# A hybrid decoder step in float32 pairs: attention scores of two heads in two row tiles of TensorE, and q and k spilled once

## The chip, the cores and the metric

The kernel runs on one core of a Trainium2 chip. The metric is the device time of one launch in microseconds (us), as the median of repeated runs. A run that was profiled also has a span, from its first to its last instruction, and a trace of every instruction on the five engines: TensorE (PE in the profile, PEld for its weight loads), VectorE (DVE), ScalarE (ACT), GpSimd (POOL) and SyncE (SP), which here only issues DMAs.

## The reference, cut to what matters

One layer of a decoder is computed for a prompt of 1024 positions and for 8 samples of 8 new positions: an RMSNorm, one input projection that is split into a convolution branch and 12 attention heads of 64 channels, the heads' attention, an output projection, a convolutional feed-forward block and a last norm. The part that the change touches is the attention of the prompt: each head attends in three dilated windows, and the three outputs are merged by their softmax denominators.

```python
DILATED_GROUPS = ((128, 1), (512, 4), (2048, 16))
...
    s = jnp.einsum('brnqhd,brnkhd->brnhqk', qs, kk) * SCALE
    ...
    s = jnp.where(mask[None, None, :, None], s, NEG_INF)
    o, lse = softmax_attend(s, vv, 'brnhqk,brnkhd->brnhqd')
...
def merge_dilation_groups(outs, lses, dtype):
    w = jax.nn.softmax(jnp.stack(lses), axis=0)
    return jnp.sum(w[..., None] * jnp.stack(outs), axis=0).astype(dtype)
```

## The kernel before

All large products run on TensorE in float32r, a single-pass form. To keep float32 accuracy each operand is split into a rounded part and the rest (`hi` and `lo`), and a product is made of three: hi by hi, hi by lo, lo by hi (`gemm`, lines 154 to 171, whose products are lines 167 to 169). Weights are loaded raw, rounded on ScalarE and subtracted on GpSimd (`load_w`, line 134).

The 12 heads are handled as 6 pairs, because a pair fills the 128 partitions. `project` (line 354) makes q, k and v of a pair with three `gemm`s and puts them into DRAM. The first three pairs are projected in a first stage (to about 246 us) together with the samples' attention for these pairs; in the stage that follows (to about 640 us) the prompt's attention, the projections of pairs 3 to 5, the samples' attention for these and the first parts of the output projection run interleaved; the feed-forward block follows (to about 1400 us) and then the last norm. `HEADS`, `SHEADS` and `PARTS` say after which head which other piece is emitted. The final order on each engine is set by a scheduler in the compiler, which is given the program and places the instructions; one engine then works strictly through its own list.

For the prompt, `prompt_part` (line 401) splits q and k on ScalarE (lines 386, 389) and VectorE (lines 387, 390) and writes hi and lo to DRAM as separate arrays (line 410). `load_head` (line 514) reads one head back. Its q tile has the 64 channels of q's hi part in partitions 0 to 63 and of its lo part in 64 to 127; a k tile has the same 64 channels twice, once for k's hi part (`kk` of part 0) and once for its lo part. So one product over 128 partitions gives (q hi + q lo) by k hi, a second gives (q hi + q lo) by k lo, and two products make the score. GpSimd makes a permuted copy `qw` of q for the near window (line 521).

`scores` (line 561) makes, for one head and one half `u` of the positions, 8 score blocks: 4 for the far windows (classes c of 256 positions) and 4 for the near window, each of 128 queries by 128 or 256 keys, with the two products at line 574 into a PSUM bank named `s` (two banks). VectorE adds the mask and takes the minimum out of PSUM (line 578) into `y`. `exchange` (line 543) brings the minima of near and far into each other's order with one float32 product (line 552). `weighted` (line 607) takes exponentials on ScalarE (line 615), transposes them on TensorE (line 642) and multiplies by v (line 659): `o` has two column tiles, 64 columns of the array for the near and 64 for the far product. Products of plain float32 (lines 552 and 659, not the transposes) run as two passes and stand twice in the trace. `prompt_heads` (line 683) makes the scores of one half of a head and then, in `finish`, the weighted sums of the half before it.

The tiles lie in SBUF pools with a fixed number of buffers: `WB` for rounded weights, `ZA` for general tiles of the first two stages, `KB` for k, `QB` for q and for qw, `YB` for y, `HB`, and `XR` for raw rows of the output projection.

Of the kernel before, what the change touches and what calls it, by code (L numbers as in the profile page):

```python
# [17 lines left out]
F32 = mybir.dt.float32  # L18
F32R = mybir.dt.float32r
# [4 lines left out]
P = 128  # L24
# [23 lines left out]
TB, WB, ZA, ZF, GA = 5, 5, 4, 10, 2  # L48
KB, VB, QB, YB, HB, UB, PT = 4, 2, 2, 7, 5, 2, 2
# [3 lines left out]
HEADS = (0, 5, 8)  # L53
SHEADS = (0,10,11)
# [3 lines left out]
XR = 3  # L58
# [14 lines left out]
def trunk_kernel(tc, xT, w_in, w_out, w_gate, w_up, w_down, par, kc, vc, sa, sf, pmask, smask,  # L73
                 yT, kT, vT, ca, cas, cf):
    nc = tc.nc
    with (
# [277 lines left out]
        def project(p, pump):  # L354
            W = [load_w(w_in[4 + 6 * c + p], KT, nc.gpsimd) for c in range(3)]
            dq = dp.tile([2, P, S], F32, name=nm("dq"))
            dk = dp.tile([2, P, S], F32, name=nm("dk"))
# [25 lines left out]
            def split_qk(c, hi, lo, cols):  # L383
                x = xs[c][:, cols]
                if c == 0:
                    nc.scalar.activation(hi, x, AF.Copy, scale=-0.125)
                    nc.vector.scalar_tensor_tensor(lo, x, -0.125, hi.bitcast(F32), op0=ALU.mult, op1=ALU.subtract)
                else:
                    nc.scalar.activation(hi, x, AF.Copy)
                    nc.vector.tensor_sub(lo, x, hi.bitcast(F32))  # L390

# [120 lines left out]
        loaded, values = {}, {}  # L512

        def load_head(p, hd):
            dq, dk, dv = spill[p][0]
            q = zt("P", "Q", QB, "qs", S, F32R)
            rows = slice(hd * 64, hd * 64 + 64)
            for part in range(2):
                nc.sync.dma_start(q[part * 64:part * 64 + 64].bitcast(F32), dq[part, rows])
            qw = zt("P", "Q", QB, "qw", S, F32R)  # L520
            nc.gpsimd.tensor_copy(qw.rearrange("p (n c j) -> p n c j", c=4, j=32),
                                  q.bitcast(F32).rearrange("p (c n j) -> p n c j", c=4, j=32))
            ks = []
            for part in range(2):
                t = zt("P", "K", KB, "kk", S, F32R)
                for half in range(2):
                    nc.sync.dma_start(t[half * 64:half * 64 + 64].bitcast(F32), dk[part, rows])
                ks.append(t)
            if hd == 0:
                vf = zt("P", "V", VB, "vf", S).rearrange("p (t d) -> p t d", d=P)  # L530
                nc.sync.dma_start(vf, dv.rearrange("(t p) d -> p t d", p=P))
                vw = zt("P", "V", VB, "vw", S).rearrange("p (t d) -> p t d", d=P)
                for c in range(4):
                    nc.sync.dma_start(vw[32 * c:32 * c + 32],
                                      dv[c * 256:c * 256 + 256].rearrange("(t p) d -> p t d", p=32))
                values[p] = vf, vw
            loaded[p, hd] = q, qw, ks
# [23 lines left out]
        def scores(p, hd, u):  # L561

            q, qw, ks = loaded[p, hd]
            kw = [k.rearrange("p (c n j) -> p n c j", c=4, j=32) for k in ks]
            st = tiny("st", 8)
            near, far = [], []

            def some(jobs):
                ps = bank("P", "s", 2)
                y = zt("P", "Y", YB, "y", 512)  # L570
                o = 0
                for (qq, k, mask, n, c) in jobs:
                    for a in range(2):
                        nc.tensor.matmul(ps[:, o:o + n], qq, k[a], start=(a == 0), stop=(a == 1))  # L574
                    o += n
                o = 0
                for (qq, k, mask, n, c) in jobs:
                    nc.vector.tensor_tensor_reduce(out=y[:, o:o + n], in0=ps[:, o:o + n], in1=mask, op0=ALU.add,  # L578
                                                   op1=ALU.min, scale=1.0, scalar=3e38, accum_out=st[:, c:c + 1])
                    (near if c < 4 else far).append(y[:, o:o + n])  # L580
                    o += n

            jobs = []
            for c in range(4):
                n = P * (u + 1)
                jobs.append((q[:, c * 256 + u * P:c * 256 + u * P + P], [k[:, c * 256:c * 256 + n] for k in ks],
                             pmk[:, 512 - n:512], n, 4 + c))
            if u == 0:
                some(jobs)
            else:  # L590
                some(jobs[:2])
                some(jobs[2:])
            jobs = []
            for i in range(4):
                nb = 4 * u + i
                n = 2 if nb else 1
                jobs.append((qw[:, nb * P:nb * P + P], [k[:, nb + 1 - n:nb + 1] for k in kw],
                             pmk[:, 256 - n * P:256], n * P, i))
            some(jobs[:2])
# [456 lines left out]
```

## Time and profile before

| | |
|---|---|
| median of 3 runs | 1440.18 us (1439.54 to 1449.22) |
| the profiled execution | 1440.49 us, its span 1438.7 us |
| mean granted TensorE clock | 0.987 of full speed |
| TensorE busy | 1391.2 us, 97% of the span |
| VectorE, ScalarE, GpSimd busy | 817.3, 430.1 and 344.5 us |
| moved by DMA | 161.64 MB, mean 112 GB/s |

In rows of the profile, `out<-in` names the tile that is written and those that are read, with buffer numbers left out, and L574 is line 574 of the kernel. Products are pipelined: a product's own duration is longer than the time from its start to the start of the next, so busy times of lines on PE can't be added up as cost; the distance between starts is the cost. In a timeline, a row stands for a run of like instructions: its start, the time to the end of the last, and their count.

### The profile page before, as it was taken

To read this page: it belongs to the slowest core of one execution; us is meant where nothing else is said; L and a number is where in the kernel's file an instruction comes from. 1 tells how busy PE (TensorE), PEld (TensorE's weight loads), DVE (VectorE), ACT (ScalarE), POOL (GpSimd) and SP (SyncE) were. 2 spreads that over 40 slices of the span, in tenths; PEclk is the share of its full clock that TensorE was granted. 3 is DMA by queue.
4 is the path that set the end of the run, shared out by engine and by line. 5 is a ranking of instruction groups with operands and counts; after the bars stand their busy time and mean duration, and the time that the engine had idled before them with its cause. 6 is when DMAs were issued, how large, how long until landed. Compare 5 with 4: busy or idle time off the path is not lost.

```text
span 1438.7 us, 23412 instructions
## 1 busy us (share of the span) xinstructions
PE 1391.2 (97%) x9408; PEld 1327.0 (92%) x9408; DVE 817.3 (57%) x1631; ACT 430.1 (30%) x887; POOL 344.5 (24%) x297
## 2 busy tenths in 40 slices
PE   7989999999999999999999999999999999999995
PEld 7989889999977778999999999999999999999995
DVE  7398695566674666586534534534544544544467
ACT  5312111557564564252111111111111111111134
POOL 3221112010010016132223223223223223232235
PEclk9999999999999999999999999999999999999997
DMA  7237676656698785221112012012011011120203
GB/s 270 61 131 266 223 261 195 189 159 178 174 273 251 214 241 204 82 75 38 31 43 66 25 43 73 18 48 68 18 56 60 18 57 37 41 70 11 70 29 125
DMA packets 75340, 161.64 MB, mean 112 GB/s; under 512 B 12000, under 2 KB 46176, under 8 KB 75232
## 3 DMA queue, kind: packets, MB, share of 16 engines
q1 hardware_dynamic: 75232, 160.15, 36.2%
q8 instruction: 74, 1.21, 0.3%
q14 instruction: 34, 0.28, 0.1%
HBM read 128.32 MB, written 31.81 MB: 111 GB/s over the span
## 4 chain that ended last, share of the span: by engine, by line
PE 84%; DVE 9%; DMA 4%; issue 1%; ACT 1%; SPq 1%; POOL 1%; POOLq 0%; DVEq 0%; ACTq 0%
PE g L167 23%; PE g L169 23%; PE g L168 22%; DVE cacc L326 4%; PE o L659 3%; PE s L574 3%; PE t L642 2%; DVE cacc L328 1%; DMA kk<-dk 1%; PE ss L493 1%; DVE qkv L374 1%; DMA cr<-in_kc 1%; DVE xl L228 1%; PE ss L467 1%; PE g L930 1%
## 5 line engine op out<-in xcount | busy, mean ns | idle before, releaser
L167 PE MATMUL g<-xh,wh 128*128 128x384 f32 x1528 | 502.2, 329 | 1.7 <-DVE x L779 1.7
L168 PE MATMUL g<-xl,wh 128*128 128x384 f32 x1528 | 501.0, 328 | 0.0
L169 PE MATMUL g<-xh,wl 128*128 128x384 f32 x1528 | 498.8, 328 | 0.0
L143 POOL TENSOR_TENSOR wl<-wr,wh 128x1024 fp32r<-128x1024 f32 (+3 forms) x148 | 243.4, 1645 | 880.2 <-PE g L169 742.5
L141 ACT ACTIVATE wh<-wr 128x1024 fp32r<-128x1024 f32 (+3 forms) x150 | 112.8, 752 | 602.1 <-PE g L169 481.1
L167 PEld LDWEIGHTS g<-xh,wh 128*128 128x128 f32 x1528 | 288.0, 189 | 3.4 <-ACT wh L141 1.9
L169 PEld LDWEIGHTS g<-xh,wl 128*128 128x128 f32 x1528 | 287.6, 188 | 2.0 <-issue 1.8
L168 PEld LDWEIGHTS g<-xl,wh 128*128 128x128 f32 x1528 | 288.1, 189 | 1.1 <-issue 1.0
L886 DVE TENSOR_TENSOR x<-g,x 128x384 f32<-128x384 f32 x168 | 89.4, 534 | 117.6 <-PE g L169 115.6
L168 PE MATMUL g<-al,wh 128*128 128x384 f32 (+1 forms) x456 | 149.5, 328 | 0.0
L167 PE MATMUL g<-ah,wh 128*128 128x384 f32 (+1 forms) x456 | 149.5, 328 | 0.0
L169 PE MATMUL g<-ah,wl 128*128 128x384 f32 (+1 forms) x456 | 147.3, 328 | 0.0
L833 DVE TENSOR_TENSOR gb<-g,rb 128x384 f32<-128x384 f32 (+1 forms) x66 | 33.6, 512 | 139.5 <-PE g L169 134.7
L615 ACT ACTIVATE y<-y,m 128x128 f32<-128x128 f32 (+1 forms) x192 | 88.4, 463 | 33.7 <-DVE m L603 33.7
L855 DVE TENSOR_TENSOR u<-g,rb 128x384 f32<-128x384 f32 (+1 forms) x66 | 35.1, 533 | 109.8 <-PE g L169 109.8
L578 DVE CUSTOM_DVE_ANT_0 y<-s,pmk 128x128 f32<-128x128 f32 (+1 forms) x192 | 63.9, 378 | 43.1 <-PE s L574 34.1
L167 PEld LDWEIGHTS g<-ah,wh 128*128 128x128 f32 x456 | 85.8, 188 | 0.0
L168 PEld LDWEIGHTS g<-al,wh 128*128 128x128 f32 x456 | 85.7, 188 | 0.0
L169 PEld LDWEIGHTS g<-ah,wl 128*128 128x128 f32 x456 | 85.5, 188 | 0.0
L326 DVE SCALAR_TENSOR_TENSOR cacc<-gp,prm,cacc 128x1024 f32<-128x1024 f32 x60 | 79.9, 1332 | 0.1
L374 DVE TENSOR_TENSOR qkv<-g,rb 128x384 f32<-128x384 f32 (+1 forms) x53 | 41.1, 775 | 46.1 <-PE g L169 46.0
L167 PE MATMUL g<-mh,wh 128*128 128x384 f32 (+1 forms) x192 | 64.1, 345 | 1.7 <-ACT mh L237 1.7
(197 smaller groups left out, 1925.1 us busy)
## 6 DMA issues: line engine op xcount, KB each, us to landing
cr<-in_kc SPq DMA_DIRECT2D x24, 768.0 KB, 8.7
cr<-in_vc SPq DMA_DIRECT2D x24, 768.0 KB, 7.1
kk<-dk SPq DMA_DIRECT2D x48, 256.0 KB, 7.1
wr<-in_w_in SPq DMA_DIRECT2D x22, 512.0 KB, 5.0
wr<-in_w_gate SPq DMA_DIRECT2D x22, 512.0 KB, 3.5
wr<-in_w_up SPq DMA_DIRECT2D x22, 512.0 KB, 3.5
wr<-in_w_down SPq DMA_DIRECT2D x40, 192.0 KB, 2.3
qs<-dq SPq DMA_DIRECT2D x24, 256.0 KB, 4.1
```

The source lines that it names most:

```text
L141: nc.scalar.activation(hi, raw, AF.Copy)
L143: lo_eng.tensor_sub(lo, raw, hi.bitcast(F32))
L167: nc.tensor.matmul(ps[c], whi[:, k, :], xh[:, t0:t0 + n], start=(k == 0), stop=False)
L168: nc.tensor.matmul(ps[c], whi[:, k, :], xl[:, t0:t0 + n], start=False, stop=False)
L169: nc.tensor.matmul(ps[c], wlo[:, k, :], xh[:, t0:t0 + n], start=False, stop=(k == nk - 1))
L326: eng.scalar_tensor_tensor(acc[:, :S], gp[:, j:j + S], col(w0 + j), acc[:, :S], op0=ALU.mult, op1=ALU.add)
L374: nc.vector.tensor_mul(by_class(x)[:, t0 // 4:(t0 + m) // 4, :], ps[:, :m].rearrange("p (j c) -> p j c", c=4), R[:, t0:t0 + m].rearrange(" ...
L574: nc.tensor.matmul(ps[:, o:o + n], qq, k[a], start=(a == 0), stop=(a == 1))
L578: nc.vector.tensor_tensor_reduce(out=y[:, o:o + n], in0=ps[:, o:o + n], in1=mask, op0=ALU.add, op1=ALU.min, scale=1.0, scalar=3e38, accum_ ...
L615: nc.scalar.activation(y, y, AF.Exp, bias=m[:, 4 * g + i:4 * g + i + 1], scale=-1.0, accum_out=den[:, g, 2 * hd + u, i:i + 1])
L659: done[x].append(nc.tensor.matmul(dst, v, m, start=not done[x], stop=(left[x] == 0)).ins)
L886: nc.vector.tensor_add(x[:, t0:t0 + n], ps[:, :n], x[:, t0:t0 + n])
```

## The change

The spill. `prompt_part` no longer splits: q and k of a pair go to DRAM once, as they are, 512 KB each. The split is made where they are read: the new `open_pair` reads both heads of a pair at once into 128 partitions (head 0 in partitions 0 to 63, head 1 in 64 to 127), rounds q and k on ScalarE, makes q's lo part on VectorE and k's on GpSimd, in place of the raw tile, and makes two permuted copies (of q hi and q lo) on GpSimd, as many as before for two heads. The raw q of the next pair is read ahead (`load_qk`); `RB = 3` raw tiles allow this and no more.

The scores. A unit of work is now one half `u` of the positions for both heads, instead of one head. Each block has three products per head (q hi by k hi, q hi by k lo, q lo by k hi) over 64 partitions: head 0 uses the upper 64 rows of the array, head 1 the lower 64, and each writes its own bank. The code writes the two heads' products alternately. The two `s` banks, which were two successive blocks of one head, are now the two heads of one block. `exchange` works for two heads at once, so it is called 12 times instead of 24 for the minima.

The pools: `WB` 5 to 4, `ZA` 4 to 3, `XR` 3 to 2, `HB` 5 to 4, `YB` 7 to 10; k and q's own pools give way to 4 tiles `Q` and 3 tiles `R`. `UNITS` and `SUNITS` have the numbers of `HEADS` and `SHEADS` but for one.

```diff
-            dq = dp.tile([2, P, S], F32, name=nm("dq"))
-            dk = dp.tile([2, P, S], F32, name=nm("dk"))
+            dq = dp.tile([P, S], F32, name=nm("dq"))
+            dk = dp.tile([P, S], F32, name=nm("dk"))
...
-                    hi, lo = zbig("qkh", F32R, S), zbig("qkl", F32R, S)
-                    split_qk(c, hi, lo, slice(0, S))
-                if c < 2:
+                    nc.sync.dma_start((dq, dk)[c], x[:, :S])
...
-                    for part, t in ((0, hi), (1, lo)):
-                        nc.sync.dma_start((dq, dk)[c][part], t.bitcast(F32))
...
+        def load_qk(p, which):
+            t = raw[p, which] = zt("P", "R", RB, "qk"[which] + "l", S, F32R)
+            nc.sync.dma_start(t.bitcast(F32), spill[p][0][which])
+        def open_pair(p):
+            parts = []
+            for which, c in ((0, -0.125), (1, 1.0)):
+                if (p, which) not in raw:
+                    load_qk(p, which)
+                t = raw.pop((p, which))
+                x = t.bitcast(F32)
+                hi = zt("P", "Q", 4, "qk"[which] + "h", S, F32R)
+                nc.scalar.activation(hi, x, AF.Copy, scale=c)
+                if which == 0:
+                    nc.vector.scalar_tensor_tensor(t, x, c, hi.bitcast(F32), op0=ALU.mult, op1=ALU.subtract)
+                else:
+                    nc.gpsimd.tensor_sub(t, x, hi.bitcast(F32))
+                parts.append((hi, t))
+            blocks = [zt("P", "Q", 4, "qw", S, F32R) for _ in range(2)]
...
-        def scores(p, hd, u):
+        def scores(p, u):
...
-                    for a in range(2):
-                        nc.tensor.matmul(ps[:, o:o + n], qq, k[a], start=(a == 0), stop=(a == 1))
+                ps = [bank("P", "s", 2) for _ in range(2)]
...
+                    for a, (q, k) in enumerate(passes[g]):
+                        for hd in range(2):
+                            r = slice(hd * 64, hd * 64 + 64)
+                            nc.tensor.matmul(ps[hd][:, o:o + n], qq(q[r]), kk(k[r]), start=(a == 0), stop=(a == 2))
...
-            r = exchange(st[:, None, 0:4], st[:, None, 4:8], 1)
+            r = exchange(st[:, 0], st[:, 1], 2)
```

What the scheduler makes of it on TensorE is seen at two places. The first is in the first pair, among the far blocks of its second half. Before, the two products of a block (k's hi part in `kk_2293`, its lo part in `kk_2296`) stand together, and projection products (`g`) and transposes (`t`) follow:

```order
L574 MATMUL s_2369<-kk_2293,qs_2288 128x256
L574 MATMUL s_2369<-kk_2296,qs_2288 128x256
L169 MATMUL g_3347<-xh_152,wl_3301 128x384
L167 MATMUL g_3347<-xh_156,wh_3299 128x384
L642 MATMUL t_2414<-ident,y_2322 128x128
L168 MATMUL g_3347<-xl_158,wh_3299 128x384
```

In the changed kernel `s_2361` is the bank of head 0 for these blocks and `s_2362` that of head 1, and `s_2381` is head 0's bank of the next two blocks:

```order
L574 MATMUL s_2362<-kh_2255,qh_2250 128x256
L574 MATMUL s_2362<-kl_2253,qh_2250 128x256
L574 MATMUL s_2362<-kh_2255,ql_2248 128x256
L169 MATMUL g_3366<-xh_136,wl_3218 128x320
L646 MATMUL t_2462<-ident,y_2322 128x128
L167 MATMUL g_3366<-xh_140,wh_3216 128x320
L574 MATMUL s_2381<-kh_2255,qh_2250 128x256
L574 MATMUL s_2381<-kl_2253,qh_2250 128x256
L574 MATMUL s_2381<-kh_2255,ql_2248 128x256
```

The two heads' products don't alternate here: the six of `s_2361` (two blocks, three products each) stand 16 other products ahead of the six of `s_2362`, and `s_2381` follows after three others. The second place is the start of the first pair, its far blocks of the first half, where they do alternate, as the code has them:

```order
L574 MATMUL s_2272<-kl_2253,qh_2250 128x128
L574 MATMUL s_2273<-kl_2253,qh_2250 128x128
L574 MATMUL s_2272<-kh_2255,ql_2248 128x128
L574 MATMUL s_2273<-kh_2255,ql_2248 128x128
L574 MATMUL s_2272<-kh_2255,qh_2250 128x128
L574 MATMUL s_2273<-kh_2255,qh_2250 128x128
```

Counted over the whole list, before there are 384 score products in 80 uninterrupted runs, 55 of them of four; now there are 576 in 72 runs. Where one score product follows another, 184 times it is of the other head and 320 times of the same. The number of places where neighbours on TensorE use the array in different shapes (128 rows by 128 columns, two row halves, or two or four column tiles) is 266 before and 368 now.

More of the change, by code (lines that the diff above doesn't have):

```diff
@@ L507, in sample_attention @@
             nc.sync.dma_start(mixed[2 + p][:, S:N], osm)
[L512 to L537, printed above, removed]
@@ L794, in trunk_kernel @@
         masks = sample_masks("U")
[L795 to L796 removed]
+        for p, upto in zip(range(NS1, NP), SUNITS):
+            prompt_units(i, upto)
             i = max(i, upto)
             sample_attention(p, "U", masks)
[L799 removed]
+        prompt_units(i, 2 * NP)
         finish()
```

123 lines of the change are left out of this document (63 added, 60 removed).

## The prediction

> **What bounds the kernel now.** I read the page first.
>
> ```profile
> span 1438.7 us, 23412 instructions
> PE 1391.2 (97%) x9408; PEld 1327.0 (92%) x9408; DVE 817.3 (57%) x1631; ACT 430.1 (30%) x887; POOL 344.5 (24%) x297
> PE   7989999999999999999999999999999999999995
> PEclk9999999999999999999999999999999999999997
> DMA  7237676656698785221112012012011011120203
> PE 84%; DVE 9%; DMA 4%; issue 1%; ACT 1%; SPq 1%; POOL 1%; POOLq 0%; DVEq 0%; ACTq 0%
> ```
>
> TensorE (PE) is busy in every slice but the first and last, and it is 84% of the chain that ended last. DMA is heavy only until slice 16. The busy times by stage (columns: stretch, length, PE, PEld, DVE, ACT, POOL, clock, DMA share, GB/s) say where the change falls:
>
> ```profile
> 0.00:246.00 246.00, 228.61 (x1655) 213.52 (x1656) 182.19 (x264) 66.61 (x96) 52.45 (x29) 0.98 0.58 200
> 246.00:640.00 394.00, 380.79 (x2944) 333.00 (x2943) 251.23 (x815) 211.97 (x581) 73.43 (x51) 0.99 0.66 189
> 640.00:1400.00 760.00, 760.00 (x4657) 759.61 (x4656) 356.11 (x492) 135.26 (x170) 199.34 (x195) 1.00 0.14 44
> ```
>
> All score products lie in the middle stretch. There PE is idle for 394.0 - 380.8 = 13 us in all, VectorE works 64% of the time and DMA 66%. So the time of this stretch is the work on PE plus a few waits, which the waits of PE name:
>
> ```profile
> PE g L398 <- DVE qkv L378: 7.2, 2, 4.2
> PE o L659 <- DMA vw<-dv: 2.9, 1, 2.9
> PE s L574 <- DMA qs<-dq: 2.6, 1, 2.6
> ...
> PE s L574 <- DMA kk<-dk: 0.9, 1, 0.9
> ```
>
> What the change gains off PE can repay at most such waits; what it adds on PE is paid in full.
>
> **The products.** Before, there are these four groups, 120 products of 128 columns and 264 of 256:
>
> ```profile
> L574 PE MATMUL s<-kk,qw 128*128 128x256 f32 x168 | 30.1, 298 | 0.0
> L574 PE MATMUL s<-kk,qs 128*128 128x256 f32 x96 | 16.5, 296 | 0.0
> L574 PE MATMUL s<-kk,qs 128*128 128x128 f32 x96 | 13.9, 283 | 3.6 <-DMA qs<-dq 2.6 <-DMA kk<-dk 0.9
> L574 PE MATMUL s<-kk,qw 128*128 128x128 f32 x24 | 4.8, 276 | 0.0
> ```
>
> Their durations overlap; the cost is the distance of starts, read from the timeline of PE:
>
> ```profile
> 262.90 0.63 PE L574 MATMUL s<-kk,qs 128*128 128x256 f32 x4
> 263.37 0.34 PE L169 MATMUL g<-xh,wl 128*128 128x384 f32 x1
> 263.54 0.34 PE L167 MATMUL g<-xh,wh 128*128 128x384 f32 x1
> ...
> 264.00 0.64 PE L574 MATMUL s<-kk,qw 128*128 128x256 f32 x4
> 264.48 0.38 PE L642 MATMUL t<-ident,y 128*128 128x128 f32 x2
> ...
> 297.04 0.75 PE L574 MATMUL s<-kk,qs 128*128 128x128 f32 x5
> 297.63 0.39 PE L167 MATMUL g<-xh,wh 128*128 128x384 f32 x1
> ```
>
> Four of 256 columns take 0.47 to 0.48 us, 0.118 each. Five of 128 take 0.59, and within the run (0.75 less one duration of 0.28, over four) 0.117; I take 0.112, since the first distance holds the change from the neighbour. Half the columns save next to nothing. Before: 120 x 0.112 + 264 x 0.118 = 44.6 us.
>
> Now the number is 576, 180 of 128 columns and 396 of 256. If no two ran together they would cost 180 x 0.112 + 396 x 0.118 = 66.9 us; if every pair did, half of it, 33.5. No product in the trace uses two row halves side by side, so I read the nearest thing, the column tiles of `o`:
>
> ```profile
> 296.20 0.38 PE L659 MATMUL o<-ph,vw 128*64 128x256 f32 x1
> 296.21 0.38 PE L659 MATMUL o<-ph,vf 128*64 128x128 f32 x2
> 296.42 0.38 PE L659 MATMUL o<-ph,vw 128*64 128x256 f32 x1
> 296.43 0.38 PE L659 MATMUL o<-ph,vf 128*64 128x128 f32 x2
> 296.63 0.38 PE L659 MATMUL o<-ph,vw 128*64 128x256 f32 x1
> 296.65 0.38 PE L659 MATMUL o<-ph,vf 128*64 128x128 f32 x2
> 296.96 0.33 PE L642 MATMUL t<-ident,y 128*128 128x128 f32 x1
> ```
>
> The second tile starts 0.01 us after the first, and in 0.22 us one tile does 256 columns while the other does twice 128. Tiles do run together, weight loads included. I take this over to row halves: two products of different heads that are neighbours in the list cost one.
>
> But mostly they aren't neighbours. In the list as compiled only 184 of the 504 places where a score product follows another change the head; the usual form is six of one head, other work, six of the other, or the two sixes in a row. With starts in list order, a product can overlap only with a neighbour: going through the list with 0.112 and 0.118, a start 0.01 after the one ahead and each half busy for its own product, 105 of the 576 vanish beside another and the sum is 55.1 us. If a half could take several products ahead of those that wait for the other half, a run of six and six would fold, but not across the work between them: 47.2 us. So the term is 55.1 - 44.6 = +10.5 us, with the ends +2.6 and +22.3. I choose the middle value because in `o` each tile's next product also comes just when list order allows it.
>
> The Trainium skill, page "TensorE: Matmul & The Clock Gate", section "Part 3: Packing small matmuls — row/col tiling", says that products start and end strictly in program order and that different row groups overlap, with a measured 3.07 times for four row tiles. By that rule the term is the same +10.5 and the end of +22.3 falls away; no run here shows row tiles yet.
>
> **The change of shape.** In the last rows above, two passes of `vf` take 0.22 us (296.21 to 296.43) while `o` goes on, but 0.31 (296.65 to 296.96) when a full-array transpose follows: 0.09 us for a change of shape. The list has 368 such places in place of 266: 102 x 0.09 = +9.2 us. I take the same for a change to row halves; the bounds are 0 (such a change is free) and 0.12 (the step from the full array to `o` is somewhat dearer): 0 to +12.
>
> **The exchange.** 12 of the 24 small float32 products go, two passes each, at the distance of one short product: 24 x 0.11 = -2.6 us. The VectorE work around it shrinks too, but VectorE is not the bound here.
>
> **The DMA.** A pair's q and k were written in 4 x 512 KB and read in 8 x 256 KB for k and 4 x 256 KB for q; now they are written and read in 2 x 512 KB each:
>
> ```profile
> kk<-dk SPq DMA_DIRECT2D x48, 256.0 KB, 7.1
> qs<-dq SPq DMA_DIRECT2D x24, 256.0 KB, 4.1
> dq<-qkh SPq DMA_DIRECT2D x6, 512.0 KB, 3.6
> ```
>
> That is 1 MB less written and 2 MB less read, over six pairs 18 MB. That is off the chain but for 2.9 + 2.6 + 0.9 = 6.4 us of PE's waits. I take half, -3, because `vw` and `vf` stay as they are and still share the queue with the 768 KB loads of the samples; the ends are 0 and -6.4.
>
> **The moved split.** It is the same work for two heads, done once per pair just before the scores:
>
> ```profile
> L389 ACT ACTIVATE qkh<-qkv 128x1024 fp32r<-128x1024 f32 x6 | 6.3, 1052 | 8.6 <-DVE qkv L378 4.7 <-DVE qkv L374 3.8
> L390 DVE TENSOR_TENSOR qkl<-qkv,qkh 128x1024 fp32r<-128x1024 f32 x6 | 7.9, 1318 | 2.3 <-ACT qkh L389 2.3
> L143 POOL TENSOR_TENSOR wl<-wr,wh 128x1024 fp32r<-128x1024 f32 x65 | 158.5, 2439 | 481.2 <-PE g L169 463.9 <-PE r L268 8.4 <-ACT wh L141 4.8
> L521 POOL CAST qw<-qs 128x1024 fp32r<-128x1024 f32 x12 | 12.5, 1040 | 150.9 <-DMA qs<-dq 66.4 <-PE t L642 43.3 <-PE g L169 24.0
> ```
>
> k's lo part, on VectorE for 1.3 us before, now takes 2.4 on GpSimd. From k's landing to the first product that reads k lo: 1.05 (ACT) + 2.44 (POOL), and up to 2 x 1.04 for the copies queued ahead, 3.5 to 5.6 us. On PE 20 to 49 other products stand between the first score product of a pair and that one; at 0.17 us (263.37 to 263.54 is the usual step of `g`) that is 3.4 to 8.3 us. So it is hidden, narrowly at the pair with 20; what is queued behind a late one on POOL are the weights' lo parts, and PE waits for those. I take 0, and up to +6 for six openings of 1 us. Fewer weight buffers (4, so no rounded part of a third product ahead) cost nothing while a projection of 72 products at 0.17 us covers 1.05 + 2.44; in the shortest output and down products it may cost 0 to +2. The waits for VectorE at line 398 (7.2 us) stay, since the convolution steps fill the room that the splits leave.
>
> **The sum.** +10.5 + 9.2 - 2.6 - 3 = +14.1 us on the profiled execution's 1440.5 us: 1454.6 us. The median of the runs shown, 1440.18, is within 0.3 us of it.
>
> **The rivals.**
>
> *The halves don't overlap.* The two heads' weight loads could go one after the other.
>
> ```profile
> L574 PEld LDWEIGHTS s<-kk,qs 128*128 128x128 f32 x192 | 25.1, 191 | 5.6 <-issue 5.1 <-DVE qkv L378 0.2 <-DVE xf L555 0.2
> ```
>
> For it: half the columns save nothing, so something other than columns sets 0.112, and each product has a load of 0.191 us. Against: the tiles of `o` load beside each other. 66.9 in place of 55.1 is 11.8 more: 1466.4 us. The same page of the Trainium skill, section "LDWEIGHTS (loading the stationary operand)", says that a load's time goes by its columns and not its rows, so 64 rows shorten no load; by the section cited above the loads of two row groups overlap all the same, which gives the forecast.
>
> *A half runs ahead of the other.* If PE holds six products for one half while it starts the other half's, the runs of six and six fold: 47.2 in place of 55.1, 7.9 less, 1446.7 us. It decides from a depth of six. For it: `o` doesn't exclude it. Against: most sixes have other work between them.
>
> *Not slower: it does as the code says,* every pair side by side, because PE starts a later score product past the work between: 33.5 in place of 55.1, 21.6 less, 1433.0 us. It decides from the point at which the products fall to 41.0 us (44.6 - 9.2 + 2.6 + 3), that is, at 223 of the 288 pairs side by side. The list, with 105, speaks against it.
>
> **Chances.** The forecast 0.5 (1446 to 1463), no overlap 0.2, run ahead 0.2, as the code says 0.1. A measurement of this kernel can tell about 1%, 14.4 us, from no change. The forecast lies at that edge and gives half of its 0.5 to slower; with 0.2 of the first rival that is 0.45. Faster by over 1% is half of the last rival, 0.05; within 1%, 0.5. The range reaches to the first two rivals and halfway to the third: 1438 to 1468 us.
>
> **What would show it.** In the new profile: L574 with 576 products of 64 rows by 128 columns; neighbours of different heads starting about 0.01 us apart and neighbours of the same head 0.11 apart; 0.09 us at each change to and from them; PE's waits for `qs`, `kk` gone and no wait of s for POOL over 1 us; the stretch from 246 us to the feed-forward block longer by about 14 us and the others as before. I am wrong if s products of two heads with work between them overlap, if heads in alternation start 0.11 apart, or if the middle stretch is not PE-bound any more.

## The result, and the profile after

| | us (median) | range |
|---|---|---|
| before | 1439.86 | 1439.28 to 1449.22, 4 runs |
| after | 1464.34 | 1461.48 to 1468.52, 4 runs |

The changed kernel is slower: 1.0155 times the time before, 95% interval 1.0113 to 1.0196, or 24.5 us. The profiled execution took 1465.51 us, its span is 1463.7; before it was 1438.7, so the two traces differ by 25.0 us.

The page of the kernel after, the rows that answer to those shown of before:

```profile
span 1463.7 us, 23379 instructions
PE 1417.3 (97%) x9576; PEld 1337.0 (91%) x9576; DVE 812.3 (55%) x1553; ACT 428.2 (29%) x886; POOL 354.2 (24%) x303
PEclk9999999989999999999999999999999999999997
DMA  7236656212286447231102112012012011020203
PE 89%; DVE 7%; DMA 1%; issue 1%; POOL 1%; ACT 1%; SPq 0%; POOLq 0%; DVEq 0%; ACTq 0%
```

PE is 89% of the chain that ended last in place of 84, and DMA 1% in place of 4: the transfers have left the path, and PE is busy for 26 us more. Busy times by stage (columns as before):

```profile
0.00:246.00 246.00, 226.65 (x1646) 211.55 (x1647) 171.30 (x256) 58.98 (x88) 52.49 (x30) 0.97 0.53 185
246.00:640.00 394.00, 384.80 (x2979) 321.65 (x2978) 215.44 (x717) 202.57 (x572) 77.63 (x51) 0.97 0.46 145
640.00:1420.00 780.00, 779.04 (x4759) 777.93 (x4758) 394.81 (x510) 147.86 (x182) 202.80 (x199) 1.00 0.15 46
```

In the middle stretch PE is idle for 9 us in place of 13 and the DMA share fell from 0.66 to 0.46, yet the work that ended before 640 us now reaches beyond it. The granted clock of the stretch went from 0.99 to 0.97. PE's waits (us in total, times, longest; ahead of these rows stand two that the change doesn't touch, 10.3 and 8.9 us, 9.6 and 8.9 before):

```profile
...
PE g L389 <- DVE qkv L378: 8.0, 2, 5.2
PE g L167 <- ACT mh L237: 3.1, 1, 3.1
PE s L574 <- DVE st L580: 1.7, 2, 1.5
PE g L169 <- POOL wl L143: 1.0, 2, 0.6
```

No wait for `qs`, `kk` or `vw` is left, and the score products never wait for GpSimd. Now two blocks of one head, which share a bank, six score products, on PE's timeline (start, duration):

```profile
280.04 0.31 PE L169 MATMUL g<-xh,wl 128*128 128x320 f32 x1
280.19 0.31 PE L167 MATMUL g<-xh,wh 128*128 128x320 f32 x1
280.33 0.30 PE L168 MATMUL g<-xl,wh 128*128 128x320 f32 x1
280.57 0.38 PE L574 MATMUL s<-kh,qh 64*128 64x256 f32 x1
280.79 0.28 PE L574 MATMUL s<-kl,qh 64*128 64x256 f32 x1
280.91 0.28 PE L574 MATMUL s<-kh,ql 64*128 64x256 f32 x1
...
281.27 0.28 PE L574 MATMUL s<-kh,ql 64*128 64x256 f32 x1
281.47 0.42 PE L169 MATMUL g<-xh,wl 128*128 128x320 f32 x1
281.73 0.27 PE L646 MATMUL t<-ident,y 128*128 128x128 f32 x1
```

Read the distances of starts. `g` steps by 0.15 us; the first score product comes 0.24 after the last `g`, 0.09 late. But the second score product comes 0.22 after the first, where the later ones come 0.12 apart: another 0.10. On the way out it is the same: `g` starts 0.20 after the last score product, and the instruction behind it 0.26 later in place of 0.15. So **a change of shape is paid twice**, at the first product and again at the second, about 0.19 us in all here. Over the trace the medians are 94 and 102 ns at 53 entries from full-array products, and 88 and 105 ns at 50 exits.

The prediction's sum, measured. From both traces I took every distance of starts on PE. A product's own time is the usual step of its kind at full clock (0.11 us for 128 columns, 0.12 for 256, 0.17 for 384; of one that starts within 0.06 us of its neighbour, only that). What a product takes beyond it goes to half clock if it starts in a stretch at a granted clock of 0.5 (the tail, the last 18 to 19 us of both kernels, is left out), else to waits if it is over 0.45 us, else to the change of shape if the shape changes just ahead of or behind it. A short wait that falls on such a place is therefore counted as a change of shape; what a change costs by itself, the first experiment measures:

| us on PE, from first to last product | before | after | difference | predicted |
|---|---|---|---|---|
| score products, own time | 44.7 | 51.7 | +7.0 | +10.5 |
| changes of shape (266, then 368) | 30.1 | 48.2 | +18.1 | +9.2 |
| exchange products, own time | 5.0 | 3.6 | -1.4 | -2.6 |
| waits | 26.0 | 24.4 | -1.6 | -3 |
| lost at half clock, the tail not counted | 10.1 | 15.1 | +5.0 | 0 |
| all other | 1304.8 | 1302.0 | -2.8 | 0 |
| sum | 1420.7 | 1445.0 | +24.3 | +14.1 |

The theory to test: the change of shape is dear, and the products, the spill and the waits are not. Its rivals: the halves do not share the array; the order of the list alone is at fault; the loss sits in the spill, or in the smaller pools.

### The profile page after: what moved, and what is told of

The parts are those of the page before. It is cut to its first block, busy times and chain, and to the rows that moved or that the text cites. A ratio compares the mean times of both kernels' runs of the same rounds, so it can differ in the third digit from the quotient of the medians.

```text
span 1463.7 us, 23379 instructions
## 1 busy us (share of the span) xinstructions
PE 1417.3 (97%) x9576; PEld 1337.0 (91%) x9576; DVE 812.3 (55%) x1553; ACT 428.2 (29%) x886; POOL 354.2 (24%) x303
## 4 chain that ended last, share of the span: by engine, by line
PE 89%; DVE 7%; DMA 1%; issue 1%; POOL 1%; ACT 1%; SPq 0%; POOLq 0%; DVEq 0%; ACTq 0%
PE g L167 24%; PE g L169 23%; PE g L168 23%; PE s L574 4%; PE o L663 3%; DVE cacc L326 3%; PE t L646 3%; PE ss L480 1%; PE ss L454 1%; DVE cacc L328 1%; DVE qkv L374 1%; PE g L933 1%; PE g L934 1%; PE g L935 1%; PE g L404 0%
## 5 line engine op out<-in xcount | busy, mean ns | idle before, releaser
L143 POOL TENSOR_TENSOR wl<-wr,wh 128x1024 fp32r<-128x1024 f32 (+3 forms) x148 | 257.2, 1738 | 877.0 <-ACT wh L141 830.5
L580 DVE CUSTOM_DVE_ANT_0 y<-s,pmk 128x256 f32<-128x256 f32 (+1 forms) x192 | 63.0, 379 | 72.4 <-PE s L574 48.1
L849 DVE SCALAR_TENSOR_TENSOR fc<-gb,prm,fc 128x1104 f32<-128x1104 f32 x44 | 87.9, 1997 | 1.5
L326 DVE SCALAR_TENSOR_TENSOR cacc<-gp,prm,cacc 128x1024 f32<-128x1024 f32 x60 | 84.4, 1407 | 0.1
```

The source lines that it names most:

```text
L143: lo_eng.tensor_sub(lo, raw, hi.bitcast(F32))
L326: eng.scalar_tensor_tensor(acc[:, :S], gp[:, j:j + S], col(w0 + j), acc[:, :S], op0=ALU.mult, op1=ALU.add)
L580: nc.vector.tensor_tensor_reduce(out=y[:, o:o + n], in0=ps[hd][:, o:o + n], in1=mask, op0=ALU.add, op1=ALU.min, scale=1.0, scalar=3e38, ac ...
L849: nc.vector.scalar_tensor_tensor(cvt[:, :W], gb[:, i:i + W], col(C_FW + 3 * j + i), cvt[:, :W], op0=ALU.mult, op1=ALU.add)
```

## Experiments

### What a change of shape costs, and how far a half runs ahead

Groups of small products stand between six full products of 384 columns, six times each.

```python
PATTERNS = {"six": "a" * 6, "one": "a", "twelve": "a" * 12, "six_six": "a" * 6 + "b" * 6,
            "three_three": ("a" * 3 + "b" * 3) * 2, "turns": "ab" * 6, "full": "f" * 6,
            "long_six": "A" * 6, "long_turns": "AB" * 6, "long_six_six": "A" * 6 + "B" * 6,
...
m = {"s": 384, "f": 128, "a": 128, "b": 128, "A": 256, "B": 256}[c]
r = {"a": H[0], "b": H[1]}.get(c.lower(), slice(0, P))
nc.tensor.matmul(ps[c.lower()][:, :m], w[r, o:o + P], data[s][r, :m], start=True, stop=True)
```

> Leaves out the whole computation: it is a row of TensorE products alone, groups of small ones between full-array products of 384 columns (0.16 us each), each group six times; a and b are products of partitions 0-63 and 64-127 with 128 columns (A and B with 256). Theory (a change to or from row tiles costs about 0.2 us, half of it at the second product behind the change; two row tiles of one pair run together; the queue runs ahead by two or three products): the single a costs 0.11 us and 0.3 to 0.4 more, six a 0.67 and 0.3 to 0.4 more, six pairs in turn no more than six a; six a and then six b 1.4 in place of 1.7 us; six a, three full, six b pays the change twice. Rival 1 (0.09 us a change, as the prediction has it): 0.18 more for every group. Rival 2 (weight loads of the two halves in turn): six pairs in turn cost 1.3 us and more, as much as six a and then six b. Rival 3 (free run-ahead): six a then six b cost as little as six pairs in turn.

One group of six pairs in turn on PE's timeline (`d_turns`):

```profile
92.75 0.34 PE L49 MATMUL ps_s<-d_sep,wt 128*128 128x384 f32 x1
93.01 0.32 PE L49 MATMUL ps_a<-d_turns,wt 64*128 64x128 f32 x1
93.02 0.32 PE L49 MATMUL ps_b<-d_turns,wt 64*128 64x128 f32 x1
93.18 0.27 PE L49 MATMUL ps_a<-d_turns,wt 64*128 64x128 f32 x1
93.18 0.27 PE L49 MATMUL ps_b<-d_turns,wt 64*128 64x128 f32 x1
93.29 0.27 PE L49 MATMUL ps_a<-d_turns,wt 64*128 64x128 f32 x1
93.29 0.27 PE L49 MATMUL ps_b<-d_turns,wt 64*128 64x128 f32 x1
...
93.62 0.27 PE L49 MATMUL ps_a<-d_turns,wt 64*128 64x128 f32 x1
93.63 0.27 PE L49 MATMUL ps_b<-d_turns,wt 64*128 64x128 f32 x1
93.83 1.32 PE L49 MATMUL ps_s<-d_sep,wt 128*128 128x384 f32 x6
```

The two halves start within 0.01 us of each other and a pair takes 0.11 us, weight loads included. What a group adds (from the last full product ahead to the second one behind, less two usual steps of 0.175 us; medians):

| group | us |
|---|---|
| six full products of 128 columns | 0.676 |
| one of a half; six; twelve | 0.45; 1.01; 1.68 |
| six pairs in turn; three, three, three, three | 1.02; 1.02 |
| six and then six of the other half | 1.30 |
| 256 columns: six; six pairs in turn; six and then six | 1.10; 1.11; 1.45 |

Six of one half cost 1.01 where six full products cost 0.68: a run of them costs **0.34 us beyond its products**, in and out together, and one lone product 0.45 in place of 0.11. The theory holds, except that it expected 1.4 us for six and six. The 0.18 of the first rival, weight loads in turn, and free run-ahead all fall: in turn costs no more than one half alone, and six and six cost 0.28 more than in turn. A half does run ahead, by little: in six and six the first product of b starts with the third of a, past three that wait (`d_six_six`; in the row of three a's the third starts at 66.81):

```profile
66.27 0.34 PE L49 MATMUL ps_s<-d_sep,wt 128*128 128x384 f32 x1
66.53 0.55 PE L49 MATMUL ps_a<-d_six_six,wt 64*128 64x128 f32 x3
66.82 0.32 PE L49 MATMUL ps_b<-d_six_six,wt 64*128 64x128 f32 x1
66.92 0.27 PE L49 MATMUL ps_a<-d_six_six,wt 64*128 64x128 f32 x1
```

In the same way three and three fold altogether.

### The two heads' banks freed together

If the list separates the heads because their PSUM banks come free at different times, one tile of two banks must bring the pairs side by side.

```diff
+        def two_banks():
+            return zone["Pps"].tile([P, 1024], F32, tag="s", name=nm("s"), bufs=1)
...
-                ps = [bank("P", "s", 2) for _ in range(2)]
+                both = two_banks()
+                ps = [both[:, :512], both[:, 512:]]
```

(The exchange takes its bank from the same tile.)

> The changed kernel with one PSUM tile of two banks for both heads, so that both heads' banks come free in the same moment; nothing is left out. Theory (the list separates the heads because the two banks come free at different times; what is lost is the lone halves and the changes to and from them): nearly all of the 288 pairs alternate, 49 runs of row products in place of 72, so products 33 to 36 us in place of 53 and 23 runs fewer at 0.39 us, together 26 to 29 us less, less 2 to 8 us of waits because the next block can't start while the DVE reads the last: 1438 to 1446 us. Rival 1 (the halves do not share the array, so order is nothing): 1460 to 1466. Rival 2 (the single pair of banks costs a DVE eviction of about 1 us in most of the 49 runs): 1460 and more.

Measured: 1455.31 us (1453.33 to 1456.96, 4 runs), 1.0112 times before, interval 1.0084 to 1.0140. Faster than the changed kernel by 9 us, and still slower than before, so the sum of the theory was at least 9 us too low. Of the 288 pairs 287 start within 0.04 us of each other, where the changed kernel has 140, so rival 1 falls; rival 2 falls because the waits for VectorE at the score products are 1.1 us in all. Two blocks of both heads on its timeline:

```profile
283.73 0.34 PE L169 MATMUL g<-xh,wl 128*128 128x384 f32 x1
283.90 0.34 PE L167 MATMUL g<-xh,wh 128*128 128x384 f32 x1
284.17 0.39 PE L578 MATMUL s<-kh,qh 64*128 64x256 f32 x2
284.39 0.28 PE L578 MATMUL s<-kl,qh 64*128 64x256 f32 x2
284.51 0.28 PE L578 MATMUL s<-kh,ql 64*128 64x256 f32 x2
...
284.87 0.28 PE L578 MATMUL s<-kh,ql 64*128 64x256 f32 x2
285.08 0.44 PE L168 MATMUL g<-xl,wh 128*128 128x384 f32 x1
285.36 0.34 PE L169 MATMUL g<-xh,wl 128*128 128x384 f32 x1
```

Twelve products in six steps. Without the block the last `g` shown would start two steps of 0.17 behind 283.90, at 284.24; it starts at 285.36. So two blocks of both heads cost 1.12 us even with every pair side by side. Before, the four full-array products of one head took 0.47 (262.90 to 263.37 in the prediction's rows), 0.94 for both heads. And a head alone, as in the rows at 280.57, costs 1.1 for its two blocks, both heads 2.2. **The break-even that the prediction put at 223 pairs does not exist at such a place:** the three products in place of two and the two changes eat the gain when all are paired.

By the table's rule the products' own time is now 34.9 us, 9.8 less than before, the changes 40.7, 10.6 more: nothing is gained on balance. Most of the 12 us by which its trace is longer than that of before are waits, 9.8 us more. The largest that are new or longer:

```profile
PE g L167 <- ACT mh L237: 7.7, 1, 7.7
PE g L169 <- POOL wl L143: 5.7, 3, 4.7
PE o L667 <- ACT ph L656: 3.5, 4, 1.8
```

`mh` is the rounded operand of the output product, and the wait for it was 1.7 us before. PE's timeline has the transposes of the last normalisation and then nothing until `mh` is there: no product of the output projection was left to fill the time. What makes the other two longer was not tested.

### The spill without the row tiles, and the pools

The first keeps the full-array products of before and its heads one by one, spills q and k once and splits them at the reading. It isn't the spill alone: it also has `WB`, `ZA` and `XR` of the changed kernel (4, 3 and 2). The second is before with the changed kernel's `WB`, `YB`, `HB` and `XR`; `ZA` stays at 4 in it.

```diff
+            raw = zt("P", "R", RB, "ql", S), zt("P", "K", KB, "kl", S, F32R)
+            for t, d in zip(raw, (dq, dk)):
+                for half in range(2):
+                    nc.sync.dma_start(t[half * 64:half * 64 + 64].bitcast(F32), d[rows])
...
+            nc.scalar.activation(q, ql, AF.Copy, scale=-0.125)
+            nc.vector.scalar_tensor_tensor(q[64:], ql[64:], -0.125, q[64:].bitcast(F32), op0=ALU.mult, op1=ALU.subtract)
```

> The kernel before with its two full-array products per block, but with q and k spilled once in float32 and split when they are read, head by head; nothing is left out. Theory (the spill half of the change is harmless and takes away the DMA waits of 6.4 us; all the loss is in the row tiles): 1432 to 1439 us, with no wait on qs, kk or vw. Rival (the openings on ACT, DVE and POOL come late and PE waits for them, or crowd the evictions): 1442 us or more, with PE waits on ACT, DVE or POOL at the score products.

```diff
-TB, WB, ZA, ZF, GA = 5, 5, 4, 10, 2
-KB, VB, QB, YB, HB, UB, PT = 4, 2, 2, 7, 5, 2, 2
+TB, WB, ZA, ZF, GA = 5, 4, 4, 10, 2
+KB, VB, QB, YB, HB, UB, PT = 4, 2, 2, 10, 4, 2, 2
...
-XR = 3
+XR = 2
```

> The kernel before with the pool sizes of the changed one for weights, staging, y and ph (4, 2, 10 and 4 buffers); nothing is left out. Theory (pool sizes are not where the time went): 1437 to 1443 us. Rival (four weight buffers in place of five make PE wait for weights through the dense stages): 1446 us and more, spread over the whole span.

Measured: the spill 1443.75 us, ratio 1.0024 (1.0003 to 1.0045); the pools 1443.39, ratio 1.0030 (1.0005 to 1.0054), just above the range of its theory; 10 runs each, beside 19 of before with a median of 1440.08. Each costs some 3.5 us, and the two share the smaller `WB` and `XR`; neither is where 24 us went. The spill took away the waits for `qs`, `kk` and `vw` (6.4 us), as expected, and gained nothing; my range of 1432 to 1439 was wrong. Among the waits that its trace has in their place are:

```profile
PE ss L454 <- DMA cr<-in_kc: 3.0, 1, 3.0
PE g L169 <- POOL wl L143: 2.9, 3, 2.0
```

Whether these come from the spill or from the smaller pools the run doesn't separate: with the pools alone PE waits 3.6 us for `cr` too, in place of 0.7 before (`cr` holds the samples' cached keys and values).

### One change alone: rows without a second half

Before, with one edit: each of the 384 score products contracts over 64 partitions, so the low part of q is left out. No other engine's work changes and nothing runs beside them.

```diff
-                        nc.tensor.matmul(ps[:, o:o + n], qq, k[a], start=(a == 0), stop=(a == 1))
+                        nc.tensor.matmul(ps[:, o:o + n], qq[:64], k[a][:64], start=(a == 0), stop=(a == 1))
```

> The kernel before with one thing changed: each of its 384 score products contracts over the first 64 partitions of its operands in place of all 128. It leaves out the terms with the low part of q; products, banks, loads and, but for a few places, the order are those of before, so that only the change of shape to and from the score products is added, around some 80 runs of them, with no second half beside them. Theory (a run of row products costs about 0.34 us beyond its products, and half-clock stretches get longer where such products stand): 27 us more and up to 6 for the clock, 1463 to 1476 us. Rival 1 (0.09 us at each change and nothing after it, as the prediction has it): 15 us more, 1452 to 1459. Rival 2 (shape costs nothing, and the loss of the changed kernel is in its order and waits): 1437 to 1444.

Measured: 1457.13 us (1455.65 to 1461.09, 4 runs), ratio 1.0121 (1.0090 to 1.0152), 15.7 us more. By the total rival 1 is right and the theory wrong. The trace says otherwise of the mechanism: 389 changes of shape in place of 266 took 53.0 us in place of 30.1, 22.9 more for 123 changes, 0.19 each, which is the theory's price and not 0.09. The span rose by less, because the waits fell from 26.0 to 21.7 us and other parts with them; PE's idle time in the middle stretch shows it, 6.9 us in place of 13:

```profile
246.00:640.00 394.00, 387.09 (x2854) 323.05 (x2853) 232.67 (x802) 204.00 (x573) 67.89 (x50) 0.99 0.64 185
```

I had also counted 80 runs at the full 0.34, where some of them had stood beside another shape before and paid already. So about a third of what is added on PE here doesn't reach the span; most of it comes out of waits (4.3 us) and of time at half clock.

### A third of the products away

The changed kernel without the third product.

```diff
-                    for a, (q, k) in enumerate(passes[g]):
+                    for a, (q, k) in enumerate(passes[g][:2]):
...
-                            nc.tensor.matmul(ps[hd][:, o:o + n], qq(q[r]), kk(k[r]), start=(a == 0), stop=(a == 2))
+                            nc.tensor.matmul(ps[hd][:, o:o + n], qq(q[r]), kk(k[r]), start=(a == 0), stop=(a == 1))
```

> The changed kernel without the third product of each score (the low part of q with the high part of k): it leaves out a third of the products, 192 of 576, and the values are those of the remaining two. The list makes 76 runs of row products in place of 72. Theory (the loss is not in the products: their sum falls to about 36 us, 9 under that of before, while the changes of shape, 76 runs at 0.34 us beyond their products, and the waits stay): 1447 to 1456 us, still above before. Rival (the products are what the change costs, each a slot of 0.11 us): 1432 to 1443 us, at or under before.

Measured: 1472.42 us (1469.08 to 1474.23, 4 runs), ratio 1.0217 (1.0185 to 1.0250): slower than the changed kernel with all its products. Both numbers were wrong, the rival's by 30 us, mine by 16. The list falls apart further: of 192 pairs only 22 run side by side, so the products' own time is 42.4 us and not 36. Against the changed kernel that is 9.3 us less, but waits cost 4.1 more, the half clock 5.1 and the changes 1.6:

```profile
PE g L167 <- ACT mh L237: 9.8, 2, 7.4
...
PE o L663 <- ACT ph L652: 2.9, 3, 1.2
```

One half-clock stretch, from 398.5 us, lasts 17.1 us. So 9.3 us less of products don't make the kernel faster, and the rival's time is 30 us off. The test is not a clean one, since this list pairs fewer products than the changed kernel's; why it comes out with more waits I did not take apart further.

### Work kept for the end

The two-bank kernel with the output product cut in other parts, so that PE has work left behind the last normalisation.

```diff
-PARTS = (3, 3, 2)
+PARTS = (3, 2, 1, 2)
```

> The kernel with one two-bank tile for both heads and its output product cut into 3, 2, 1 and 2 row blocks in place of 3, 3 and 2, so that some 10 us of it are left for TensorE behind the last normalisation; nothing is left out. Theory (of what the two-bank kernel lost against its sum, the 7.7 us wait for the last row blocks and the half clock behind it are the largest part): 1440 to 1447 us, no wait of more than 2 us on mh. Rival (the attention chain itself ends late, and work kept for later only moves the wait into the attention): 1451 us or more with new waits on st, ph or y.

```diff
-PARTS = (3, 3, 2)
+PARTS = (3, 3, 1, 1)
```

> The same with the output product cut into 3, 3, 1 and 1 row blocks, so that the next to last pair's block is what fills the time behind the last normalisation; nothing is left out. Theory: 1441 to 1449 us, the wait on mh under 3 us. Rival (as above): 1451 us or more.

Measured: 3, 2, 1, 2 takes 1452.91 us (6 runs), ratio 1.0085 (1.0057 to 1.0112); 3, 3, 1, 1 takes 1467.05, ratio 1.0189 (1.0161 to 1.0217). The first still waits 4.8 us for `mh`, the second 4.6 and for something new:

```profile
PE g L167 <- DVE x L786: 9.2, 6, 4.2
```

With one row block a chunk of the output is three products, 0.5 us, and VectorE's addition of a chunk takes 0.54 us (median of 72 at line 786): it becomes the bound there. Moving the filling work is no cure, as the rival said; the first is 2.4 us under the two-bank kernel, and their runs overlap. No version that I tried beats the kernel before.

### What a wait costs

In the changed kernel a wait of 1.5 us (`s` for `st`, at 316.5 us) is followed by 10.2 us at half clock. Two more kernels of products alone:

```python
nc.scalar.copy(t[:, :384], ps["s"][:, :384])
for _ in range(n_copies - 1):
    nc.scalar.copy(t[:, :384], t[:, :384].bitcast(F32))
product("s", s)
for _ in range(AFTER // (1 if kind == "s" else 6)):
    for c in (["s"] if kind == "s" else list("ssss" + "ab" * 6)):
        product(c, "sep")
```

> Leaves out the whole computation: TensorE products alone, in two parts. First groups as in the first such row: four and four, five and five products of the two halves, three times two and two, six and six with one full product between, and full-row products of 64 and of 32 columns of the array. Theory (the queue runs ahead by three, and a change costs 0.09 us and about as much again at the second product): four and four run all but one pair together, five and five all but two, two and two all; the groups of 64 and 32 columns pay the same change as the halves. Rival (the price belongs to the row tiles alone): these groups cost 0.2 us or less beyond their products. Second part: dense products of 384 columns, then a wait of TensorE for 1, 2, 3, 4 or 6 ACT copies of 384 columns (about 0.5 us each), then 19 us dense again, five times each; and the same with pairs of halves mixed into the dense part. Theory (a wait of more than about 1 us is followed by 3.4 us or more at half clock, so that it costs about twice its length): half-clock stretches behind the waits of 1.5 us and more, none behind those of 0.5. Rival 1 (the halves bring the half clock): half-clock stretches in the second kind and few in the first. Rival 2 (neither): the clock stays at 1 in both.

```python
MIXES = {"full": "s" * 10, "small": "ssss" + "f" * 12, "turns": "ssss" + "ab" * 6, "alone": "ssss" + "a" * 6,
         "sparse": "s" * 12 + "ab" * 6}
```

> Leaves out the whole computation: TensorE products alone. A wait of TensorE of about 2 or 3 us on ACT copies, then about 50 us of one mix of products, then 21 us of dense full products of 384 columns, which bring the clock back; three times for each mix and wait. Mixes: full products alone; four full and twelve full of 128 columns; four full and six pairs of halves in turn; four full and six of one half alone; twelve full and six pairs. Theory (the wait takes the clock to a half, and dense full products get it back after 3.4 us, but work that is rich in row halves and changes of shape does not): half clock for 3.4 to 6.8 us after a wait in the first mix, 3.4 to 10 us in the second and the last, and through nearly all of the 50 us in the third and fourth. Rival 1 (any small products hold it down, not the halves): the second mix stays at half clock as long as the third. Rival 2 (the length is set by the wait alone): the same length in all mixes.

The first part of the first kernel confirms the run-ahead of three, a little more than expected: four and four fold altogether (0.80 us), five and five cost 1.07. With one full product between six and six the group costs 2.08, twice a lone six: a half did not start past a full product. The groups of 64 and 32 columns of the array paid no change at all (one such product adds 0.11 us, six 0.41): there the theory is wrong and its rival right, for tiles at the array's first columns; the tiles of `o`, side by side in the kernels, do pay.

In its second part (waits given here, and in the next kernel, as the distance of starts across them, some 0.27 to 0.34 us more than PE's idle time), with dense full products, a wait of 0.9 or 1.3 us never brought the half clock, one of 1.76 us twice in five times, one of 2.63 us every time, for 3.4 us each and once 6.8. With halves mixed in, the first of the waits of 1.65 us did nothing; the second took the clock to a half and it stayed there for the remaining 513 us, although the same mix had run at full clock for some 480 us until then. Two stretches, ahead of that wait and behind it (columns: length, PE, PEld, ACT, POOL, clock, DMA share, GB/s):

```profile
1100.00:1130.00 30.00, 30.00 (x283) 24.26 (x283) 0.38 (x1) 0.00 (x0) 1.00 0.01 2
1133.00:1180.00 47.00, 47.00 (x253) 38.65 (x252) 0.00 (x0) 0.00 (x0) 0.50 0.00 1
```

The second kernel asks what holds it there. Half clock behind waits of 2.3 to 3.7 us, six of each mix: full products alone 0 to 6.8 us; four full and twelve small full products 96 to 99 us in five of six, that is, to the end of the mix; the same with pairs of halves 92 us in five of six; with one half alone 89 to 92 in five of six; twelve full and six pairs 3.4 to 10.2. The 50 us of mix so take nearly twice their time. Stretches of the small mix and of the last one (the last 16 us of the second row are full products again):

```profile
480.00:560.00 80.00, 80.00 (x335) 80.00 (x334) 0.00 (x0) 0.00 (x0) 0.50 0.00 0
...
2440.00:2500.00 60.00, 60.00 (x433) 55.47 (x432) 0.00 (x0) 0.00 (x0) 1.00 0.00 1
```

So rival 1 is right: small full-array products hold the clock down as halves do, once a wait has brought it there, and my theory that it is the halves is wrong. What in these mixes holds it stays open; with twelve full products in the mix it came back. PE is "busy" for 80 of 80 us there, and that doesn't help. The Trainium skill, page "TensorE: Matmul & The Clock Gate", section "Part 1: The HAM clock gate (the "warmup" mystery)", has the full clock return after one busy window of about 3.4 us. The full products here agree (3.4 us, at times 6.8); the mixes rich in small ones don't, for 89 to 99 us.

## Why the prediction was right in its range and wrong in a step

The 1464.34 us lie in the range of 1438 to 1468, but above the interval that the forecast itself was given (1446 to 1463); its sum, 1454.6, is 10 us too low. The time lies 2 us from the price of a rival that is false (no overlap of the halves, 1466.4), so the number alone would have pointed to the wrong mechanism. That the range held is in part luck: the changes of shape (8.9 us) and the clock (5.0) were too low, the products too high (3.5).

- **The change of shape** is the step that failed, a term mis-sized by half: 102 changes at 0.09 us, +9.2 with bounds 0 to +12, against +18.1 measured, 0.18 each. The 0.09 was read at the first product behind a change. The second half of the price falls on the product behind that, in the kernel before too: medians there are 93 ns at the first and 57 at the second product for 77 changes from `o` to full products, 93 and 105 for 37 changes from the sample products. It could have been read blind.
- **The products**: +7.0 in place of +10.5. The row tiles do run together, 0.01 us apart, as taken over from `o`, and the list decides, as said. A half runs ahead by three products, not by none and not by the six that the rival needed; 140 pairs run side by side in place of the 105 vanished products counted. The Trainium skill, page "TensorE: Matmul & The Clock Gate", section "Part 3: Packing small matmuls — row/col tiling", has products start strictly in program order. That does not hold in these runs, and neither does the sentence ahead of the prediction that an engine works strictly through its own list: products of one half start past three waiting ones of the other.
- **PE bounds the stretch, and what is added on it is paid in full**: not quite. In the rows-only kernel 22.9 us of changes cost 15 us of span; in the two-product kernel 9.3 us of products taken away came back as waits and half clock. A sum over PE's work gives the time here only because the waits moved little (-1.6).
- **The DMA waits** went altogether, 6.4 us and not half. The bytes came out as summed: 18.9 MB less moved. That was no gain: the waits as a whole fell by 1.6, and the spill without the row tiles is not faster than before.
- **The exchange**: -1.4 in place of -2.6. **The moved split** cost nothing, as said: no wait on GpSimd at the scores, 1.0 us at `wl`. Fewer weight buffers were put at 0, at most +2; the four pool sizes tried alone cost 3.3 us by the median, with an interval from 0.7 to 7.8. `UNITS` and `SUNITS` have all the numbers of `HEADS` and `SHEADS`, without the exception that the section on the change speaks of.
- **The clock** was missing from the sum: +5.0 us in these two traces. Every half-clock stretch of before but the tail lasts 3.4 us; now three last 6.8 and one, behind a wait of 1.5 us among small products, 10.2. That small products lengthen it there is argued from the last experiment, not shown in the kernel; in the rows-only kernel one stretch of four lasts 6.8 us and the others 3.4.

Of the rivals, weight loads in turn is ruled out (pairs at 0.11 us); run-ahead is real but of three; all pairs side by side was made and still lost: its price, 1433.0, had the waits fall by 3 us where they grew by 9.8, and most of its error lies there. Its products (-9.8 for -11.1) and changes of shape (+10.6 for +9.2) came out near the price, though it has 73 more changes and not 102.

The signs came out so: neighbours of different heads 0.01 us apart, of one head 0.11 to 0.12, waits for `qs` and `kk` gone, as said; "0.09 at each change" is the one that failed, and the stretch grew by some 24 us in place of 14: its first score product starts at 250.9 us in place of 249.0, the last product of the output projection at 653.0 in place of 626.8. Of the three signs of being wrong none came: a half did not start past a full product (in products alone, the 2.08 us above), pairs did not start 0.11 apart, and PE is busy for 384.8 of 394 us.

## What to carry to other kernels

Count a run of row-tiled products with its way in and out, 0.34 us here, before comparing products: a run of six pairs side by side saved less than that. Read the price of a change at the second instruction behind it as well as at the first. The list kept two tiles neighbours (287 pairs of 288) when their PSUM banks came free together; with banks of their own it was 140.

## What the runs showed of the hardware that I had not expected

- Entering or leaving 64-row tiles delays the first product behind by 0.09 us and the second by 0.05 (128 columns) to 0.10 us.
- Products of one half start past up to three waiting products of the other (four and four fold altogether, six and six in part).
- With 1.65 to 1.76 us between two starts on PE the clock fell to a half in some cases (three of seven at full clock), with 2.3 to 3.7 us in 31 of 35. Full products of 384 columns brought it back after 3.4 or 6.8 us; mixes rich in products of 128 columns didn't for 89 to 99 us and once for 513, though the same kind of mix keeps the full clock where no wait has taken it.
